# Two-layer attention and mLSTM trunk: q and k of three pieces of four turned by VectorE in 32x32 blocks and through DRAM instead of by TensorE transposes

## The chip, the cores and the metric

The kernel runs on one core of one Trainium2 chip. The metric is the device time of one execution in microseconds (us). The same kernel was run three times: the median is 1334.58 us, the runs lie between 1334.22 and 1334.67. One further execution was recorded by the hardware profiler: it took 1334.56 us, of which 1332.5 us is the span of the trace (first to last recorded instruction).

## The reference

The program is a decoder trunk of two layers over 512 tokens of 1024 channels, in float32. Each layer normalises x, multiplies it with one wide matrix, and feeds the parts to two branches: differential attention with rotary positions, and a chunkwise mLSTM. Both branches are gated, projected, merged and added to x.

```python
proj = rmsnorm(x, norm_g) @ w_in
aq, ak, av, az, bqk, bv, bi, bf, bo, bz, ga, gb = jnp.split(proj, idx, axis=-1)
q = rope(rmsnorm(two_map_heads(aq), q_norm_g), cos, sin)   # 8 heads x 2 maps x 512 tokens x 64
k = rope(rmsnorm(two_map_heads(ak), k_norm_g), cos, sin)
...
sc = jnp.einsum('bhqrd,bhkrd->bhrqk', qb, k) * scale       # causal, softmax over k, two maps r
p = jax.nn.softmax(jnp.where(causal, sc, -jnp.inf), axis=-1)
a = p[:, :, 0] - lam * p[:, :, 1]
oa = rmsnorm(a @ v, attn_norm_g) * (1 - lam_init) * silu(az)
...
u = sigmoid(ga) * (oa @ w_out_a) + sigmoid(gb) * (hb @ w_out_b)
x = x + u @ w_o
```

What the change touches is the way from `aq`, `ak` to the operands of the score product: in the projection a token is a partition, since norm and rotary turn work along a head's 64 features; in the score product the feature has to be the partition. So q and k (4 pieces `c` of two heads each, of q and k together 512 columns) are turned once in every layer.

## The kernel before

**Arithmetic.** Each float32 factor is split into a high part that TensorE takes as its reduced float32 (`wh`, `hh`) and a low rest (`wl`, `hl`); a product is three matmuls (`mm3`, L507): high by high, high by low, low by high. Weights arrive by SyncE's (SP) DMAs as pieces of 128x1024 (`load`, L480, tile `wr`); `prep` (L505) makes `wh` on ScalarE (ACT, a cast) and `wl` on VectorE (DVE, a subtraction).

**Order.** All operations are first recorded (`Recorder`, L103), then ordered by a list scheduler with its own costs and many tuned numbers (`schedule` L272, table `TUNE` L38), and then issued in that order (L441, which is why every row of the profile bears this line). What tells rows apart are the names of the tiles. `TUNE["order"]` gives the order in which the pieces of the projections reach TensorE; other numbers bias when an operation is picked.

**A piece of q and k** (`tok_piece` L708 with `h_tok` L744): for each of four tiles of 128 tokens, the tokens' columns of `hh`, `hl` are the stationary operand (128 contiguous columns) and the 512 columns of the weights move; 8 k-steps of 3 matmuls go to one PSUM tile `qk`, of which the ring `acc` has four for everything that is projected. A piece `c` holds q and k of heads 2c and 2c+1.

**After each tile** (`qk_done` L827): ACT or DVE sum the squares per head and map (`sq`, `qss`); DVE multiplies with a table of cosines and with one of sines in two halves (`ctab`, `stab`: q's and k's gains are in them) and adds (`rot`). After each second tile `rq`, the inverse root mean square, is made. `qk_back` (L883) scales the k half of `rot` by it (ACT in tiles 0 and 2 by four activations of 64 columns, DVE in tiles 1 and 3); q is not scaled, its `rq` is a factor inside the softmax.

**The turn** (`back`, L892): TensorE transposes `rot` in four 128x128 blocks into a PSUM tile `qkt`; ACT casts q's and k's high parts out of it (6 casts of 64x256) and DVE subtracts the low parts (4 of 64x256). High and low part of q lie in one tile of 128 partitions (64 and 64), k's high part twice beside `kl`, half of which is zeroed by GpSimd (POOL, a memset of 64x1024). `back` is deferred by `TUNE["qkt"]` steps after the tile.

**Scores and softmax** (`attn_head` L1161, `qk` L1165): for each head and query block j two matmuls per map give `sc`; DVE adds the causal mask, takes the maximum, multiplies it with -`rq`, and ACT makes the exponentials with `scale=rq` and that bias.

**Start.** `rope_tables` (L538) makes cosines and sines of 4x32 angles per partition from the positions (`posi`), mostly on DVE (`ang`, `rn`, `rnh`), and `layer_consts` (L634) multiplies gains into them: 4 operations for `ctab`, 4 for `stab`, each 128x128.

**Decay tables** (`decay` L1299, `expm` L1314): broadcast rows `dd` and `em` come from DRAM by SP's queue. POOL issues 16 DMAs of weights (`ws_wo`, `wt_wo`) and otherwise only memsets.

Of the kernel before, what the change touches and what calls it, by code (L numbers as in the profile page):

```python
# [42 lines left out]
    ),  # L43
    "qkt": 5,
    "gct": 15,
    "gls": 6,
    "glf": 5,
    "attn": (1, 5, 5, 8, 9, 13, 15, 16, 19, 24),
    "a0": 23,
    "ap": 18,  # L50
    "a4": 7,
    "ml": (1, 9, 11, 12, 13, 28),
# [3 lines left out]
    "margin": 72.0,  # L56
    "pemargin": 171.8,
    "wait": 333.1,
    "swpen": 701284048.1,
    "smargin": 51.6,  # L60
    "pwait": 0.8,
    "wdiff": 3673.3,
    "wsp": 4,
    "kact": (0, 2),
    "qsq": (1, 3),
    "foldA": (2, 3, 5),
    "foldM": (0, 1, 2, 3, 4, 7),
    "foldD": (0, 1, 2, 3, 4, 5, 6, 7),
# [3 lines left out]
    "acl": 12,  # L72
    "gateA": 9,
    "gateM": 0,
    "actp": (0, 2, 3),
    "m0": 218,
    "mp": 15,
    "m4": 11,
    "slots": 20,
    "bias": {'av': 27450.0, 'msp_a': -4350.0, 'wl': 2400.0, 'wo': -3700.0, 'woh': -4650.0, 'ht': 29150.0, 'taz': -4050.0, 'ga': 16050.0, 'gt': -8800.0, 'p': -300.0, 'wo1_P': 23900.0, 'out_0_dram': -5900.0, 'p5_wo': -4950.0, 'rot': 12650.0, 'dq': -4400.0, 'oa': 450.0, 'dd': 30900.0, 'num': 20100.0, 'ld': -4700.0, 'ws1_wo': -1200.0, 'gw': -1100.0, 'hl': -350.0, 'sc': -1400.0, 'uz': -3750.0, 'mk': 7250.0, 'sbz': 550.0, 'az': 10300.0, 'posi': -650.0, 'msl_d': 1650.0, 's1_wo': 1700.0, 'wob': 50.0, 'msh_d': 6450.0, 'sq': -1600.0, 'warm': 3150.0, 'bo': -400.0, 'sdl': 200.0, 'ml': 15800.0, 'fo_b': 11200.0, 'ws0_wo': -900.0, 'wt1_wo': 1300.0, 'pb': 2000.0, 'sbo': 5350.0, 'qkt': 2000.0, 'junk': 6150.0, 'ulZ': 7650.0, 'bv': 650.0, 'bqk': -1750.0, 'uh': -3950.0, 'ms_b': -1550.0, 'gi': 1000.0, 'ob': 250.0, 'uy': 1750.0, 'gcol': -750.0, 'ms': 11250.0, 'cosv': -4100.0, 'ms_a': 1450.0, 'ones': 2450.0, 'msh_b': 6650.0, 'x1d': -1650.0, 'qt': 1100.0, 'qk0_2x': -6300.0, 'fb_a': 4650.0, 'saz': 900.0, 'xr': -2300.0, 'fb_b': 900.0, 'wo0_P': 450.0, 'qk1_0x': 1950.0, 'fb_d': -5800.0, 'msh_a': 2700.0, 'ulA': -150.0, 'ang': 150.0, 'rnh': 1400.0, 'gft': 6600.0, 'gct': 200.0, 'gc': -300.0, 'mql': -1200.0, 'rows': 150.0, 'kl': -700.0, 'posf': -150.0, 'zw': 2400.0, 'qk1_2x': -3000.0, 'gf': 450.0, 'qk0_0x': -50.0, 'uhY': 7150.0, 'qs': 3050.0, 'qy': 250.0, 'ul': -500.0, 'msl_a': 2800.0, 'uhZ': 7800.0, 'lneps': -950.0, 'gm': -4350.0, 'lq': 450.0, 'x': -3700.0, 'eps': -700.0, 'sgb': 150.0, 'wr': -400.0, 'wt0_wo': -300.0, 'stab': 8000.0, 'xn': 1200.0, 'qss': 150.0, 'den': 2000.0, 'msl_b': 950.0, 'rn': -150.0, 'glf': 900.0, 'ss': 4250.0, 'bz': -100.0, 'sdh': -200.0, 'em': -250.0, 'uhB': 850.0, 'rq': 250.0, 'sinv': -1650.0},  # L80
    "drain": 251.9,
    "risk": 295.5,
    "late": 912.7,
# [19 lines left out]
class Recorder:  # L103
# [39 lines left out]
    def region(self, ap):  # L143
# [4 lines left out]
        if k not in self.regions:  # L148
            free = math.prod(k[0][1:])
            p0, np_ = ap.offset // free, pat[0][1]  # L150
# [121 lines left out]
    def schedule(self):  # L272
# [65 lines left out]
        while len(order) < n:  # L338
# [54 lines left out]
            if o["fn"] == "dma_start":  # L393
                size = 4.0
                for x in list(o["a"][0].shape):
                    size *= x
                go = s + c if e == "POOL" else s
                dma = max(dma, go) + size / self.rate(o)
                end[i] = max(dma, go) + 2000.0
# [45 lines left out]
def kernel(ctx, tc, x, pos, wp, wg, cst, par, pb, ngb, out):  # L445
# [52 lines left out]

    xcur = big.tile([P, NT, D], F32, tag="big", name="x0")
# [35 lines left out]
    cosv = cp.tile([P, NT, 32], F32, name="cosv")  # L535
    sinv = cp.tile([P, NT, 32], F32, name="sinv")

    def rope_tables():  # L538
        NF = NT * 32
# [4 lines left out]
        posf = small(NT, "posf")  # L544
# [81 lines left out]
    def layer_events(l):  # L626
# [7 lines left out]
        def layer_consts():  # L634
# [3 lines left out]
            stab = cp.tile([P, NT, 2, 64], F32, tag="stab", name=f"stab{l}")  # L638
            for i in range(2):
                g = pbt[:, B_QK + 64 * i : B_QK + 64 * i + 64]  # L640
                f8 = 8.0 if i else 1.0
                for hf in range(2):
                    gh = g[:, 32 * hf : 32 * hf + 32]
                    go = g[:, 32 * (1 - hf) : 32 * (1 - hf) + 32]
                    V.scalar_tensor_tensor(ctab[:, :, i, 32 * hf : 32 * hf + 32], cosv, f8, gh.unsqueeze(1).to_broadcast([P, NT, 32]), ALU.mult, ALU.mult)
                    V.scalar_tensor_tensor(
                        stab[:, :, i, 32 * hf : 32 * hf + 32], sinv, -f8 if hf == 0 else f8, go.unsqueeze(1).to_broadcast([P, NT, 32]), ALU.mult, ALU.mult
                    )
            st["ctab"], st["stab"] = ctab, stab
# [177 lines left out]
        def qk_done(c, tt, acc):  # L827
# [27 lines left out]
            ctab, stab = st["ctab"], st["stab"]  # L855
            V.tensor_tensor(q4, a4, ctab[:, tt].unsqueeze(2).to_broadcast([P, 2, 4, 64]), ALU.mult)
            for hf in range(2):
                o = 32 * hf
                V.tensor_tensor(
                    s4[:, :, :, o : o + 32],  # L860
                    a4[:, :, :, 32 - o : 64 - o],
                    stab[:, tt, :, o : o + 32].unsqueeze(2).to_broadcast([P, 2, 4, 32]),
                    ALU.mult,
                )
            V.tensor_tensor(rq, rq, r2, ALU.add)
            st[("rot", tt % 2)] = rq
            if tt % 2 == 0:
                return
# [13 lines left out]

        def qk_back(c, tt, rq):  # L883
            k3 = rq[:, 256:512].rearrange("p (g d) -> p g d", d=64)
            rk = st[("rq", c)][:, tt, 4:8].unsqueeze(2).to_broadcast([P, 4, 64])
            if tt in TUNE["kact"]:
                for g in range(4):
                    A.activation(k3[:, g, :], k3[:, g, :], AF.Copy, scale=st[("rq", c)][:, tt, 4 + g : 5 + g])
            else:
                V.tensor_tensor(k3, k3, rk, ALU.mult)  # L890
# [750 lines left out]
```

## Time and profile before

| what | value |
|---|---|
| median of 3 runs | 1334.58 us (1334.22 to 1334.67) |
| profiled execution / its span | 1334.56 us / 1332.5 us |
| TensorE (PE) matmuls | 1325.0 us busy, 99% of the span, x6200 |
| weight loads of TensorE (PEld) | 1095.0 us, 82% |
| VectorE (DVE) | 1018.0 us, 76% |
| ScalarE (ACT) | 907.8 us, 68% |
| GpSimd (POOL) | 36.9 us, 3% |
| bytes moved by DMA | 148.14 MB, 111 GB/s |

Busy times are those of recorded instructions. A matmul's record covers its passage through the array, so successive matmuls overlap: the rate is read from start to start, not from a record's length. "Idle before" of a group is the time its engine waited ahead of it, with the releaser of most of it.

### The profile page before, as it was taken

The page shows a single profiled execution, that of the slowest core. Times are in us where ns is not written, and L with a number is a line of the kernel's source. Part 1 is how long each engine was busy: PE and PEld are TensorE (multiplying, and loading weights), DVE is VectorE, ACT ScalarE, POOL GpSimd, SP SyncE. Part 2 cuts the span into 40 slices and gives each one's busy share as a digit, 9 for nine tenths or more (in the row PEclk, how much of TensorE's full clock was granted, in tenths as well). Part 3 has the DMA queues.
Part 4 walks back from the last instruction along what each step waited for, and adds up shares of the span by engine and source line. Part 5 has one row for each costly group of instructions (what it writes and reads, how often), then busy time and mean ns, then how long its engine had stood idle before and what let it go on. Part 6 is the DMA issues. An engine that isn't in the chain of part 4 may idle for free.

```text
span 1332.5 us, 17532 instructions
## 1 busy us (share of the span) xinstructions
PE 1325.0 (99%) x6200; PEld 1095.0 (82%) x6200; DVE 1018.0 (76%) x1846; ACT 907.8 (68%) x1836; POOL 36.9 (3%) x44
## 2 busy tenths in 40 slices
PE   9999999999999999999999999999999999999998
PEld 7888888888888888888788888888888888888886
DVE  7898899786259968755888988997852699687566
ACT  6878798877247858743667787889762489687343
POOL 1000000000000000000200000000000000000000
PEclk9999999999999999999999999999999999999999
DMA  5222222223333443554833122222332344354646
GB/s 188 87 67 78 80 83 64 91 79 99 95 103 112 149 123 113 146 155 128 248 112 95 49 95 64 79 76 83 82 112 79 128 119 141 99 135 135 170 122 182
DMA packets 51272, 148.14 MB, mean 111 GB/s; under 512 B 6096, under 2 KB 12880, under 8 KB 51184
## 3 DMA queue, kind: packets, MB, share of 16 engines
q1 hardware_dynamic: 48880, 138.63, 32.9%
q0 software_dynamic: 2304, 8.39, 3.6%
q8 instruction: 49, 0.80, 0.2%
q14 instruction: 39, 0.32, 0.1%
HBM read 142.74 MB, written 4.26 MB: 110 GB/s over the span
## 4 chain that ended last, share of the span: by engine, by line
PE 98%; ACT 1%; DMA 0%; SPq 0%; DVE 0%; issue 0%; DVEq 0%
PE qk L441 13%; PE av L441 9%; PE az L441 7%; PE bv L441 7%; PE bqk L441 7%; PE bz L441 7%; PE bo L441 7%; PE gb L441 7%; PE ga L441 7%; PE woa L441 7%; PE wob L441 7%; PE wo_P L441 6%; PE sc L441 3%; PE num L441 2%; PE ms L441 1%; PE ut L441 1%
## 5 line engine op out<-in xcount | busy, mean ns | idle before, releaser
L441 ACT CAST wh<-wr 128x1024 fp32r<-128x1024 f32 (+1 forms) x206 | 214.8, 1045 | 190.0 <-PE ga L441 36.3
L441 DVE TENSOR_TENSOR wl<-wr,wh 128x1024 fp32r<-128x1024 f32 (+1 forms) x208 | 248.9, 1200 | 99.7 <-ACT wh L441 98.9
L441 PE MATMUL qk<-wh,hh 128*128 128x512 f32 x256 | 96.1, 401 | 0.5 <-ACT hh L441 0.5
L441 PE MATMUL qk<-wh,hl 128*128 128x512 f32 x256 | 95.3, 400 | 0.1
L441 PE MATMUL qk<-wl,hh 128*128 128x512 f32 x256 | 94.8, 396 | 0.5 <-DVE wl L441 0.5
L441 ACT ACTIVATE p<-sc,mx,rq 128x128 f32<-128x128 f32 (+3 forms) x128 | 78.8, 618 | 16.2 <-DVE mx L441 15.6
L441 PE MATMUL woa<-oa,wh 128*128 128x512 f32 x256 | 87.8, 390 | 0.0
L440 ACT ACT_TABLE_LOAD x65 | 83.4, 1283 | 1.1
L441 PE MATMUL wob<-ob,wh 128*128 128x512 f32 x256 | 83.4, 389 | 0.0
L441 PEld LDWEIGHTS qk<-wl,hh 128*128 128x128 f32 x256 | 48.0, 188 | 10.2 <-DVE wl L441 0.9
L441 PEld LDWEIGHTS wob<-ob,wh 128*128 128x128 f32 x256 | 48.1, 188 | 10.1
L441 PEld LDWEIGHTS qk<-wh,hl 128*128 128x128 f32 x256 | 48.0, 188 | 10.0 <-DVE hl L441 0.4
L441 PEld LDWEIGHTS qk<-wh,hh 128*128 128x128 f32 x256 | 47.7, 188 | 10.0 <-ACT hh L441 0.9
L441 PEld LDWEIGHTS woa<-oa,wh 128*128 128x128 f32 x256 | 47.8, 188 | 9.7
L441 DVE TENSOR_REDUCE mx<-sc 128x2 f32<-128x256 f32 (+1 forms) x64 | 52.5, 821 | 1.1
L441 PE MATMUL bqk<-hh,wl 128*128 128x512 f32 x128 | 50.3, 393 | 0.0
L441 PE MATMUL bo<-hh,wl 128*128 128x512 f32 x128 | 50.2, 392 | 0.0
L441 PE MATMUL bo<-hl,wh 128*128 128x512 f32 x128 | 50.1, 391 | 0.0
L441 PE MATMUL bo<-hh,wh 128*128 128x512 f32 x128 | 50.0, 391 | 0.0
L441 PE MATMUL bqk<-hl,wh 128*128 128x512 f32 x128 | 50.0, 393 | 0.0
L441 PE MATMUL az<-hh,wh 128*128 128x512 f32 x128 | 49.8, 397 | 0.0
L441 PE MATMUL gb<-hl,wh 128*128 128x512 f32 x128 | 49.8, 392 | 0.0
(309 smaller groups left out, 3695.9 us busy)
## 6 DMA issues: line engine op xcount, KB each, us to landing
wr<-in_wp_dram SPq DMA_DIRECT2D x204, 512.0 KB, 3.5
ws_wo<-in_wp_dram POOLq DMA_DIRECT2D x12, 512.0 KB, 6.8
dd<-rows SPq DMA_DIRECT2D x16, 256.0 KB, 4.3
em<-rows SPq DMA_DIRECT2D x16, 256.0 KB, 4.0
dd<-rows SPq DMA_DIRECT2D x16, 192.0 KB, 4.8
x<-in_x_dram SPq DMA_DIRECT2D x4, 512.0 KB, 7.4
dd<-rows SPq DMA_DIRECT2D x16, 128.0 KB, 6.0
ws_wo<-in_wp_dram SPq DMA_DIRECT2D x4, 512.0 KB, 5.2
```

Of the source, the lines that this page charges most:

```text
L440: self.tc.keep_in_program_order(self.nc.scalar.preload_act_table_set(self.SET_NAME[o["load"]]))
L441: self.tc.keep_in_program_order(getattr(o["e"], o["fn"])(*o["a"], **o["k"]))
```

## The change

For pieces c = 1, 2, 3 of both layers TensorE's transposes are gone; c = 0 keeps them (`turn`).

- The stationary operand takes every fourth token (`h_perm`): partition p of tile tt is token 4p+tt. Its 128 columns lie 16 bytes apart in place of 4.
- q is scaled by `rq` as k is (`qk_back`, ACT 8 activations of 128x64 in tiles 0, 1 and 2, DVE one 128x512 in tile 3), for c = 0 too. q gets a minus sign in the tables; so the mask is subtracted, a minimum replaces the maximum, and the exponential has `scale=-1.0`: the multiplication of the maximum goes.
- DVE transposes the two 256-column halves of each `rot` in blocks of 32x32, with a strided output, into `tr0`, `tr1`, so that after four tiles 128 tokens of a feature follow each other.
- POOL's queue writes them to `scr` in DRAM (feature by token; 8 writes of 32x8x128, 128 KB each) and reads them with features on partitions: 4 reads into `re` (float32) and 6 straight into the high parts, converted on the way (64x2x512, 256 KB each). DVE subtracts 4 low parts of 64x1024.
- A second set of tables for the permuted tokens: angles, cosines and sines are made for 8x32 in place of 4x32, the first piece's tables lie in a scratch tile `tab`, the positions come in the other order by 4 small DMAs of SP. The sine product is one operation in place of two.
- The loads of `dd` and `em` go from SP's queue to POOL's.
- The order of the pieces and all tuned numbers are new (the first pieces: `qk0 av0 gate az0 qk1` before, `qk0 qk1 az0 gate av0` now); the three lists of heads whose sums of squares are folded to 64 partitions change (`foldA`, `foldM`, `foldD`). Rings `wr`, `wh`, `wl` keep their sizes.

Instructions in the program, before and after: PE 6202 and 6102, DVE 1840 and 1718, ACT 1574 and 1574, POOL 20 and 208, SP 345 and 269 (POOL and SP: DMAs and memsets).

```diff
     "order": (
-        "qk0 av0 gate az0 qk1 az1 az2 av1 qk2 az3 az4 qk3 az6 ga3 az5 ga5 ga4 ga2 az7 bqk7 bv0 bqk4 bqk1 "
+        "qk0 qk1 az0 gate av0 av1 az2 az1 qk2 az3 az4 qk3 az5 bqk7 ga6 ga5 ga7 az6 az7 ga3 bv0 bo0 ga2 "
...
-    "qkt": 5,
+    "qkt": 9,
...
+    "qq": 2,
...
-    "kact": (0, 2),
+    "kact": (0, 1, 2),
...
-    posi = cp.tile([P, NT], I32, name="posi")
+    posi = cp.tile([P, 2 * NT], I32, name="posi")
...
-        SY.dma_start(posi, pos)
+        SY.dma_start(posi[:, :NT], pos)
+        for c in range(NT):
+            SY.dma_start(posi[32 * c : 32 * c + 32, NT:], pos.rearrange("(d t) c -> c d t", t=NT)[c])
...
-        NF = NT * 32
+        NF = 2 * NT * 32
...
-        for tt in range(NT):
+        for tt in range(2 * NT):
             V.tensor_scalar(ang[:, tt * 32 : tt * 32 + 32], ct[:, C_IF : C_IF + 32], posf[:, tt : tt + 1], None, ALU.mult)
...
+            st["tabs"] = ((first[:, 0], first[:, 1]), (ctab, stab))
...
+                    for w, (tc_, ts_) in enumerate(st["tabs"]):
+                        ns = slice(w * NT, w * NT + NT)
+                        V.scalar_tensor_tensor(tc_[:, :, i, ds], cosv[:, ns], f8, gh, ALU.mult, ALU.mult)
+                        V.scalar_tensor_tensor(ts_[:, :, i, ds], sinv[:, ns], -f8 if hf == 0 else f8, go, ALU.mult, ALU.mult)
...
+        def h_perm(k, tt):
+            return st["hh"][:, k, tt::NT], st["hl"][:, k, tt::NT]
...
         def qk_back(c, tt, rq):
+            r8 = rq.rearrange("p (g d) -> p g d", d=64)
...
-                for g in range(4):
-                    A.activation(k3[:, g, :], k3[:, g, :], AF.Copy, scale=st[("rq", c)][:, tt, 4 + g : 5 + g])
+                for g in range(8):
+                    A.activation(r8[:, g, :], r8[:, g, :], AF.Copy, scale=st[("rq", c)][:, tt, g : g + 1])
...
+            for i in range(2):
+                V.transpose(st["tr"][i].rearrange("p (a r) -> p a r", r=P)[:, :, tt::NT], rq[:, 256 * i : 256 * i + 256])
+            if tt < NT - 1:
+                return
+            scr = dram.tile([S, S], F32, name=f"scr{l}_{c}")
+            for i in range(2):
+                for b in range(NT):
+                    QW.dma_start(
+                        scr[256 * i : 256 * i + 256, P * b : P * b + P].rearrange("(a b) r -> b a r", b=32),
+                        st["tr"][i][32 * b : 32 * b + 32].rearrange("p (a r) -> p a r", r=P),
+                    )
...
             def back():
-                pst = ps_tr.tile([P, 4, P], F32, tag="tr", name=f"qkt{l}_{c}_{tt}")
-                for g in range(4):
-                    T.transpose(pst[:, g, :], rq[:, g * P : (g + 1) * P], ident)
...
+                for e, q, k, kl, a, b in ((0, q0, k0, kl0, L, H), (1, q1, k1, kl1, H, L)):
+                    r = q2w(f"re{e}{l}_{c}", F32).rearrange("p (g t) -> p g t", g=2)
+                    QR.dma_start(r[a], s5[0, e])
+                    G.dma_start(q[a], s5[0, e])
+                    QR.dma_start(r[b], s5[1, e])
+                    G.dma_start(k[a], s5[1, e])
+                    G.dma_start(k[b], s5[1, e])
+                    V.tensor_tensor(q[b], r[a], q[a].bitcast(F32), ALU.subtract)
+                    V.tensor_tensor(kl[a], r[b], k[b].bitcast(F32), ALU.subtract)
...
-                V.tensor_tensor(dg, dg, mask_a.unsqueeze(1).to_broadcast([P, 2, P]), ALU.add)
+                V.tensor_tensor(dg, dg, mask_a.unsqueeze(1).to_broadcast([P, 2, P]), ALU.subtract)
...
-                V.tensor_reduce(mx, sc[:, :, :n], AX.X, ALU.max)
...
-                V.scalar_tensor_tensor(mx, mx, -1.0, rq, ALU.mult, ALU.mult)
+                V.tensor_reduce(mx, sc[:, :, :n], AX.X, ALU.min)
...
-                    SY.dma_start(dd[:, OFF[i] : OFF[i] + n], rows[h : h + 1, P * i :].to_broadcast([P, n]))
+                    G.dma_start(dd[:, OFF[i] : OFF[i] + n], rows[h : h + 1, P * i :].to_broadcast([P, n]))
...
-                SY.dma_start(em, rows[8 + h : 9 + h, :].to_broadcast([P, S]))
+                G.dma_start(em, rows[8 + h : 9 + h, :].to_broadcast([P, S]))
...
-            ps["qk%d" % c] = tok("qk", c, h_tok, qk_done)
+            ps["qk%d" % c] = tok("qk", c, h_perm if c else h_tok, qk_done)
```

With `qq` at 2 both `QW` and `QR` are POOL's queue (`G`).

The order on TensorE at the end of the first piece of layer 0, before: in the names `qk0_0_3` is layer 0, piece 0, tile 3, the number behind the last underscore counts tiles.

```order
L441 MATMUL qk0_0_3_137<-wh3_139,hl0_115 128x512
L441 MATMUL qkt0_0_0_183<-ct_94,rot0_0_0_164 128x128 x2
L441 MATMUL qk0_0_3_137<-wh3_139,hh0_114 128x512
L441 MATMUL qk0_0_3_137<-wl3_140,hh0_114 128x512
L441 MATMUL qk0_0_3_137<-wh3_139,hl0_115 128x512
L441 MATMUL av0_0_0_179<-wh4_153,hh0_114 128x512
```

The same place now.

```order
L457 MATMUL qk0_0_3_137<-wh3_139,hh0_114 128x512
L457 MATMUL qk0_0_3_137<-wl3_140,hh0_114 128x512
L457 MATMUL qk0_0_3_137<-wh3_139,hl0_115 128x512
L457 MATMUL qk0_1_0_180<-wh4_154,hh0_114 128x512
L457 MATMUL qk0_1_0_180<-wl4_155,hh0_114 128x512
```

The second piece of q and k stands where the first of v stood, and no transposes stand between the matmuls. The piece that follows still needs the first of the four PSUM tiles of `qk0_0` back.

The order on POOL around piece c = 2 of layer 0, before: between its memsets POOL issues nothing.

```order
L441 MEMSET kl00_1_279 64x1024
L441 MEMSET kl10_1_280 64x1024
L441 MEMSET kl00_2_411 64x1024
L441 MEMSET kl10_2_412 64x1024
L441 MEMSET kl00_3_492 64x1024
L441 MEMSET kl10_3_493 64x1024
```

The same place now (`qk0_2x` is the tile of q's and k's high and low parts of this piece).

```order
L457 DMA scr0_2_434<-tr00_2_423 32x8x128 x4
L457 DMA scr0_2_434<-tr10_2_424 32x8x128 x4
L457 DMA qk0_2x_412<-scr0_2_434 64x2x512 x2
L457 DMA re00_2_460<-scr0_2_434 64x2x512
L457 DMA re10_2_461<-scr0_2_434 64x2x512
L457 MEMSET kl00_3_491 64x1024
L457 MEMSET kl10_3_492 64x1024
L457 DMA re00_2_460<-scr0_2_434 64x2x512
L457 DMA qk0_2x_412<-scr0_2_434 64x2x512
L457 DMA re10_2_461<-scr0_2_434 64x2x512
L457 DMA qk0_2x_412<-scr0_2_434 64x2x512 x3
```

All 18 transfers of a piece stand in one queue, and the two memsets for the next piece between them.

More of the change, by code (lines that the diff above doesn't have):

```diff
@@ L71 @@
     "prods": 'P1 P5 P3 P6 P2 P7 P4',
[L72 to L75, printed above, removed]
+    "acl": 14,
+    "gateA": 1,
+    "gateM": 4,
+    "actp": (0, 1, 2, 3),
     "m0": 218,
[L77 to L78 removed]
+    "mp": 17,
+    "m4": 23,
     "slots": 20,
[L80 removed]
@@ L84 @@
+    "drain": 1559.5,
+    "risk": 203.8,
+    "late": 61.0,
 }
@@ L149, in region @@
             free = math.prod(k[0][1:])
+            if t.name.startswith("scr"):
+                off = [ap.offset]
+                for st, n in pat:
+                    off = [o + st * i for o in off for i in (range(n) if st > 1 else range(0, n, 32))]
+                quad = mask = 0
+                for o in off:
+                    quad |= 1 << o // free // 256
+                    mask |= 1 << o % free // 32
+                self.regions[k] = quad, mask
+                return (t.name,) + self.regions[k]
             p0, np_ = ap.offset // free, pat[0][1]
@@ L398, in schedule @@
                 dma = max(dma, go) + size / self.rate(o)
-                end[i] = max(dma, go) + 2000.0
+                end[i] = max(dma, go) + (4000.0 if o["a"][1].tensor.name.startswith("rows") else 2500.0)
             for t in o["tiles"]:
@@ new lines, in qk_back @@
+                for g in range(8):
+                    A.activation(r8[:, g, :], r8[:, g, :], AF.Copy, scale=st[("rq", c)][:, tt, g : g + 1])
+            else:
+                V.tensor_tensor(r8, r8, st[("rq", c)][:, tt, 0:8].unsqueeze(2).to_broadcast([P, 8, 64]), ALU.mult)
+            if c == 0:
+                defer(TUNE["qkt"], lambda: turn(c, tt, rq))
+                return
+            if tt == 0:
+                take(2)
+                st["tr"] = [q2w(f"tr{i}{l}_{c}", F32) for i in range(2)]
@@ L1478, in add_up, with way, wtile, src_of @@
             G.dma_start(chains[n, a], source(l, n, 1, 1 if t == "T2" else 0, a), accum_op=ALU.add)
+    per = len(layers[0][0])
+    def way(i):
+        key = pieces[i][1]
+        if key == "gate" or key[0] == "seven" and key[2] not in ("P1", "P2", "P3"):
+            return "s"
+        for w in "ab":
+            lo, hi, step, ph = TUNE["w" + w]
+            if lo <= i % per < hi and i % step in ((ph,) if isinstance(ph, int) else ph):
+                return w
+        return "s"
+    def wtile(name, dt):
+        tag = name.rstrip("0123456789")
+        return wpool.tile([P, 1024], dt, tag=tag, bufs=2 if tag == "wr" else 3, name=name)
+    def src_of(i):
+        l, key = pieces[i]
+        if key == "gate":
+            return wg[l]
+        if key[0] == "seven":
+            _, n, prod, a = key
+            return source(l, n, *{"P1": (0, 0), "P2": (1, 0), "P3": (1, 1)}[prod], a)
+        return wp[l, KIDX[key]]
     def load(i):
@@ L1510, in prep @@
         if key == "gate":
-            wh = wpool.tile([P, 1024], F32R, tag="wh", name=f"wh{i}")
+            wh = wtile(f"wh{i}", F32R)
             w4 = wh.rearrange("p (k a n) -> p k a n", k=KT, a=2)
@@ L1547 @@
             starts[i](state["t"])
-        for a in range(3):
-            load(i + a)
+        for a in range(max(3, TUNE["wahead"])):
+            if a < 3 or i + a < len(pieces) and way(i + a) == "a":
+                load(i + a)
         for a in range(TUNE["acl"] + 1):
```

150 lines of the change are left out of this document (82 added, 68 removed), and 6 rows, old and new, of the table TUNE.

## The prediction

> **What bounds the kernel now.** I read the page first: busy shares, then the chain that ended last.
>
> ```profile
> PE 1325.0 (99%) x6200; PEld 1095.0 (82%) x6200; DVE 1018.0 (76%) x1846; ACT 907.8 (68%) x1836; POOL 36.9 (3%) x44
> ...
> PE 98%; ACT 1%; DMA 0%; SPq 0%; DVE 0%; issue 0%; DVEq 0%
> ```
>
> TensorE is the chain: 98% of it. The waits of TensorE by what it waited for say how little of that is waiting:
>
> ```profile
> PE warm L441 <- DVE ml L441: 1.6, 1, 1.6
> PE qk L441 <- ACT hh L441: 0.5, 1, 0.5
> PE ht L441 <- DVE junk L441: 0.5, 2, 0.3
> PE qk L441 <- DVE wl L441: 0.5, 1, 0.5
> ```
>
> These four come to 3.1 us, all at the start. The windows of the stretches in which q and k are made and of the start (busy time of PE, PEld, DVE, ACT, POOL, then granted clock, DMA share, GB/s):
>
> ```profile
> 0.00:35.00 35.00, 31.78 (x143) 24.88 (x144) 26.79 (x73) 21.53 (x52) 4.94 (x9) 1.00 0.53 179
> 100.00:200.00 100.00, 100.00 (x492) 82.39 (x491) 89.72 (x200) 84.38 (x233) 1.90 (x2) 1.00 0.25 81
> 200.00:300.00 100.00, 100.00 (x487) 82.40 (x487) 85.32 (x183) 82.74 (x201) 1.90 (x2) 1.00 0.24 78
> ```
>
> PE never stops between 100 and 300 us at a granted clock of 1.00, DVE stands at 90% and 85% beside it. So the time is the sum of what TensorE issues, plus what it would newly wait for. What an instruction costs there is read from starts, on TensorE's timeline around a group of four transposes:
>
> ```profile
> 218.96 0.39 PE L441 MATMUL az<-hl,wh 128*128 128x512 f32 x1
> 219.19 0.40 PE L441 MATMUL az<-hh,wl 128*128 128x512 f32 x1
> 219.42 0.60 PE L441 MATMUL qkt<-ct,rot 128*128 128x128 f32 x4
> 219.78 0.48 PE L441 MATMUL az<-hh,wh 128*128 128x512 f32 x1
> 220.09 0.39 PE L441 MATMUL az<-hl,wh 128*128 128x512 f32 x1
> 220.32 0.39 PE L441 MATMUL az<-hh,wl 128*128 128x512 f32 x1
> ```
>
> A matmul of 512 columns starts 0.23 after another (218.96 to 219.19 to 219.42). From 219.19 to 220.32 lie 1.13 us with three of them (0.68) and four transposes: 0.45, or 0.112 each.
>
> **The change part by part.**
>
> *Transposes.* 128 become 32: 96 x 0.112 = 10.75 us off TensorE's queue. All of it is on the path, as nothing else holds TensorE there. Bounds by the rounding of the starts: 10.3 to 11.2.
>
> *Folded heads.* The lists of folded heads change the 512-wide matmuls with ones by -10, +4 and +2: -4 x 0.23 = -0.9.
>
> *DVE and ACT.* The rows that go and the nearest ones of what comes (mean ns of one behind the comma, or min/median/max):
>
> ```profile
> L441 ACT CAST ks<-qkt x64: 360/367/371, 106.7 to 897.8; 64x256 fp32r<-64x256 f32 x64
> L441 DVE TENSOR_TENSOR qs<-qkt,qs x32: 417/422/428, 106.3 to 897.0; 64x256 fp32r<-64x256 f32 x32
> L441 DVE SCALAR_TENSOR_TENSOR mx<-mx,rq 128x2 f32<-128x2 f32 x64 | 9.9, 155 | 0.7
> L441 ACT ACTIVATE rot<-rot,rq 128x64 f32<-128x64 f32 x64 | 17.4, 340 | 1.9 <-DVE rq L441 1.6
> L441 DVE TENSOR_TENSOR wl<-wr,wh 128x1024 fp32r<-128x1024 f32 x200 | 243.7, 1221 | 98.5 <-ACT wh L441 97.7
> L441 DVE TENSOR_TENSOR sq<-qk,stab 128x256 f32<-128x256 f32 x64 | 25.5, 416 | 0.3
> ```
>
> DVE loses 96 subtractions (40.5) and 64 products of the maximum (9.9); it gains 24 subtractions of 1024 columns by the `wl` row (29.3) and 48 block transposes of 128x256, which the trace does not have: by the nearest row of that size, `sq`, 0.42 each (20), at worst twice that for the strided output (40), at best half (10). Net about -1 us, -11 to +19. ACT loses 144 casts (52.8) and gains 128 scalings (43.5): -9. Both fit under TensorE, so I take nothing for them in the sum; what would end the cover is in the rivals.
>
> *The start.* The first piece's rotary products now wait for more tables. DVE's timeline, then TensorE's first matmul behind the first piece:
>
> ```profile
> 20.90 0.57 DVE L441 TENSOR_SCALAR ang<-ct,posf 128x32 f32<-128x32 f32 x3
> ...
> 26.13 0.29 DVE L441 SCALAR_TENSOR_TENSOR ang<-rnh,ang 128x128 f32<-128x128 f32 x1
> ...
> 30.17 0.29 DVE L441 SCALAR_TENSOR_TENSOR stab<-sinv,pb 128x128 f32<-128x128 f32 x1 [0.35 <-ACT sinv L441]
> 30.38 0.28 DVE L441 SCALAR_TENSOR_TENSOR ctab<-cosv,pb 128x128 f32<-128x128 f32 x1
> ...
> 32.39 0.75 DVE L441 TENSOR_TENSOR sq<-qk,stab 128x256 f32<-128x256 f32 x2
> 33.05 1.22 DVE L441 TENSOR_TENSOR wl<-wr,wh 128x1024 fp32r<-128x1024 f32 x1
> ```
>
> ```profile
> 36.12 0.40 PE L441 MATMUL av<-wh,hh 128*128 128x512 f32 x1
> ```
>
> Tile 0 of the first piece gave its PSUM back at 33.1, 3 us before `av` wanted it (the ring has four tiles). Ahead of that point DVE now has 4 more angle rows (0.57/3 = 0.19 each, 0.8), about 15 rows of 256 columns in place of 128 (0.42 by `sq` for 0.29: 2.0), 8 more table rows (0.20 from start to start, 1.6) and one more `wl` (1.2): 5.6 us. Release at 38.7 against 36.1: **2.6 us** of waiting, all on the path. Bounds: 0, if DVE's gaps (here 0.35) and a better place of the `wl` take it up; 5.6, if something else is late with it. The 4 small loads of positions are on SP:
>
> ```profile
> 4.54 0.60 SPq L441 DMA_DIRECT2D posi<-in_pos_dram  x1
> ...
> 11.62 7.10 SPq L441 DMA_DIRECT2D wr<-in_wp_dram  x3
> ```
>
> They add 4 x 0.60 = 2.4 us to SP's queue ahead of a weight piece that is used some 10 us after it was issued here; the cover is those 10 us, and without it 2.4 us would be paid once.
>
> *The way through DRAM.* From the last matmul of a piece, DVE ends its tail, POOL issues 18 DMAs and 2 memsets, the last read lands, DVE subtracts, and only then the first score of head 2c can start. In before, c = 2, the tail shows on TensorE's and DVE's timelines:
>
> ```profile
> 171.21 0.39 PE L441 MATMUL qk<-wh,hl 128*128 128x512 f32 x1
> ```
>
> ```profile
> 181.47 0.41 DVE L441 TENSOR_TENSOR rot<-rot,rq 128x256 f32<-128x256 f32 x1
> ```
>
> 10.7 us to the end of the last scaling; a scaling of twice the columns (+0.3) and two block transposes (0.8) make it 11.8. For POOL's DMAs there are only loads of weights, 512 KB each: POOL's timeline, the time to landing of this tile, and the table of DMA issues (last number: median us to landing):
>
> ```profile
> 560.64 1.00 POOL L441 DMA_DIRECT2D ws_wo<-in_wp_dram  x1 [143.16 <-DVE dq L441]
> 561.79 0.87 POOL L441 DMA_DIRECT2D ws_wo<-in_wp_dram  x1 [0.15 <-issue]
> ...
> 20.44 0.95 POOL L441 MEMSET kl<- 64x1024 f32 x1 [15.75 <-DVE junk L441]
> ...
> DMA to landing us min/median/max: 4.4/6.1/8.4
> ```
>
> ```profile
> ws_wo<-in_wp_dram POOLq DMA_DIRECT2D x12, 512.0 KB, 6.8
> ...
> em<-rows SPq DMA_DIRECT2D x16, 256.0 KB, 4.0
> ...
> ws_wo<-in_wp_dram SPq DMA_DIRECT2D x4, 512.0 KB, 5.2
> ```
>
> One DMA holds POOL 0.87 to 1.15 (from start to start); I take 1.01, 0.86 and the gap of 0.15. The same 512 KB take 5.2 from SP and 6.8 from POOL, 1.6 more; 256 KB take 4.0 from SP, so 5.6 from POOL. Chain: 11.8 + 17 x 1.01 + 2 x 0.95 + 5.6 + 1.3 (the subtraction) = 37.8 us. Cover on TensorE for c = 2, counted in the new order from the last `qk` matmul to the first `sc` of head 4: 154 matmuls of 512 columns (35.0) and 13 narrower ones, 2,816 columns together (1.2): 36.2. So 1.6 us late in each layer, **3.2** in both. Bounds: with 0.87 and 4.4 the chain is 34.2 and hidden (0), with 1.15 and 6.8 it is 41.4, 5.2 late, 10.4 in both. Piece 1 has a cover of some 55 us and piece 3 of 46.9: hidden, even at the upper bound. Behind the waiting subtractions DVE's queue has piece 3's sums of squares and rotary products, which hold PSUM tiles, and two `wl`; TensorE needs the first of those 28 rows after the score, so the score comes first.
>
> The Trainium skill ("DMA: Bandwidth & Descriptors", Specifications) gives first-byte latencies of about 1 us for GpSimd's path and 0.6 for SyncE's, 0.4 apart where the rows have 1.6. By the page the chain would be 36.6 and 0.4 late, and the whole time, as an estimate, 1326.3.
>
> `dd` and `em` on POOL: 80 DMAs x 1.01 = 81 us on an engine that is busy 37 of 1332; they land 1.6 later and are asked for long before use. Nothing; if issued late behind a piece's 18, a few us on DVE first.
>
> **Sum**, against the profiled execution (1334.56, 0.02 from the median): 1334.56 - 10.75 - 0.9 + 2.6 + 3.2 = **1328.7 us**. All bounds at their good end give 1322.4, all at their bad end 1339.4.
>
> **The rivals.**
>
> *A: strided weight loads are slow, slower.* The weight loads of the projection and of the transposes:
>
> ```profile
> L441 PEld LDWEIGHTS qk<-wl,hh 128*128 128x128 f32 x256 | 48.0, 188 | 10.2 <-DVE wl L441 0.9
> ```
>
> 188 ns of 227 is shown, but the four transposes at 112 ns each had a load each, so a load occupies 112 at most. It decides once a load passes 227, twice that. Three times, 336, would add 0.109 x 576 (three pieces of 96 matmuls, two layers) = 63 us: about 1391. For it: no load in the trace has that stride. Against it: the room of a factor of two. The Trainium skill ("SBUF — State Buffer", the section on the DMA port swizzle) says that SBUF has 16-byte lines, that full bandwidth needs two hits in a line and each crossing pays; at 16 bytes each value is in a line of its own. That speaks for this rival, without a size; no row here shows it. Chance 0.06.
>
> *B: POOL is late with its DMAs, slower.* A write has 256 rows of 512 bytes where `ws_wo` has 128 of 4 KB. If POOL's time goes by rows, the 8 writes take 1.73 each: 11.8 + 8 x 1.73 + 9 x 1.15 + 1.9 + 6.8 + 1.3 = 46.0, 9.8 late, 19.6 in both layers: 1325.5 + 19.6 = 1345.1. It ends above 1337.2 once a piece is 5.9 late, at 1.26 us per DMA. Against it: the order leaves 36 us of cover. Chance 0.14.
>
> *C: the gain goes to DVE or ACT.* DVE at 90% with a burst of transposes and subtractions behind a DMA wait: weights' `wl` or the `p` of the softmax come late by a fraction of a us at many places, 6 us in all: 1334.6. For: the windows. Against: DVE's and ACT's sums fall. Chance 0.14.
>
> *D: more than the sum.* No wait at the start or at piece 2, and the 3.1 us of waits at the start shrink by the new order: 1334.56 - 10.75 - 0.9 - 2 = 1321. Chance 0.06.
>
> **How the numbers follow.** The forecast has 0.60 and, by itself, a range from 1322.4 to 1331.9. 0.2% is 2.7 us, what a measurement of this kernel can tell from no change. Faster: forecast and D, 0.66. Same: C, 0.14. Slower: A and B, 0.20. The range goes from D's side, 1320, to 1342, which takes in C, the sum's bad end of 1339.4 and the milder half of B; A and the rest of B, some 0.15, are left out.
>
> **What would show it.** Right: 32 `qkt` transposes, PE at 99%; a wait of 2 to 3 us of the second piece's first matmul for a `qk` tile near 36 us; a wait of `sc` before heads 4 of 1 to 2 us on a subtraction or DMA; 0.227 from start to start in the second piece as in the first. Wrong: a longer spacing there (A); waits of over 5 us before `sc` and POOL at over 1.3 us per DMA (B); many short waits of PE on `wl`, `p` or `uh` (C).

## The result and the profile after

The changed kernel takes 1357.17 us (median of 4 runs, 1355.95 to 1360.38) against 1334.49 of the kernel before: a ratio of 1.0171, interval 1.0159 to 1.0184. It is 22.7 us slower; 1328.7 was forecast. The profiled execution took 1356.59 us and has a span of 1354.8 (before: 1332.5).

The page of the changed kernel, busy shares and the chain that ended last:

```profile
PE 1328.9 (98%) x6100; PEld 1118.2 (83%) x6100; DVE 1019.0 (75%) x1724; ACT 873.0 (64%) x1836; POOL 144.0 (11%) x232
...
PE 77%; DVE 8%; DMA 7%; ACT 5%; issue 1%; POOL 1%; SPq 0%; DVEq 0%; ACTq 0%; POOLq 0%
```

TensorE issues 100 matmuls less and is no longer the whole chain: 98% has become 77%, the rest is other engines' work that it waited for. VectorE's busy time is what it was (1018.0) and ScalarE's is lower (907.8), so neither is fuller than before; GpSimd has more to do (144.0 for 36.9), but is busy 11% only. TensorE's longest waits, by what it waited for (us in total, times, longest); all of them together come to 21.6 us, where they were 3.8 before:

```profile
PE av L457 <- ACT av L457: 3.6, 2, 2.3
PE av L457 <- DVE wl L457: 2.2, 2, 1.3
PE ga L457 <- DVE wl L457: 2.2, 2, 1.2
PE sc L457 <- DMA qk_2x<-scr: 2.0, 1, 2.0
PE warm L457 <- DVE ml L457: 1.6, 1, 1.6
PE sc L457 <- DVE kl L457: 1.6, 1, 1.6
...
PE gt L457 <- DVE sq L457: 1.2, 1, 1.2
PE ut L457 <- DVE kl L457: 1.2, 1, 1.2
```

Of these only `warm` stood there before. The waits are many, short and for different things: `sc` waits for the way through DRAM (3.6), the others for weights (`wl`), for splits of v (`av`), for the rotary work of the second piece (`sq`) and for the turn of the first (`kl` of `ut`). The windows of two of the stretches shown before (PE, PEld, DVE, ACT, POOL, clock, DMA share, GB/s):

```profile
100.00:200.00 100.00, 97.47 (x461) 84.56 (x460) 85.59 (x170) 71.35 (x188) 5.79 (x10) 1.00 0.35 93
200.00:300.00 100.00, 96.84 (x459) 82.53 (x458) 85.06 (x158) 73.39 (x192) 19.30 (x32) 1.00 0.66 154
```

TensorE stood at 100.00 in both windows and now misses 2.5 and 3.2 us, while VectorE is no busier (89.72 and 85.32 before). More is missing at the start of each layer's attention half (3.6 from 35 to 100 us, 4.2 from 700 to 800). The gated half of the first layer, 300 to 400 us, is still at 100.00.

### The profile page after: what moved, and what is told of

It reads as the page before. It is cut to its first block, busy times and chain, and to the rows that moved or that the text cites. A ratio compares the mean times of both kernels' runs of the same rounds, so it can differ in the third digit from the quotient of the medians.

```text
span 1354.8 us, 17584 instructions
## 1 busy us (share of the span) xinstructions
PE 1328.9 (98%) x6100; PEld 1118.2 (83%) x6100; DVE 1019.0 (75%) x1724; ACT 873.0 (64%) x1836; POOL 144.0 (11%) x232
## 3 DMA queue, kind: packets, MB, share of 16 engines
q1 hardware_dynamic: 37936, 123.95, 28.7%
## 4 chain that ended last, share of the span: by engine, by line
PE 77%; DVE 8%; DMA 7%; ACT 5%; issue 1%; POOL 1%; SPq 0%; DVEq 0%; ACTq 0%; POOLq 0%
PE qk L457 10%; PE bo L457 6%; PE bv L457 6%; PE av L457 6%; PE wob L457 6%; PE gb L457 6%; PE bz L457 6%; PE wo_P L457 6%; PE woa L457 5%; PE bqk L457 5%; PE ga L457 3%; DMA wr<-in_wp_dram 3%; PE az L457 2%; PE sc L457 2%; PE num L457 2%; DVE wl L457 2%
## 5 line engine op out<-in xcount | busy, mean ns | idle before, releaser
L457 ACT ACTIVATE p<-sc,mx 128x128 f32<-128x128 f32 (+3 forms) x128 | 67.5, 529 | 25.8 <-DVE mx L457 23.1
L457 PEld LDWEIGHTS qk<-wh,hh 128*128 128x128 f32 x256 | 67.2, 281 | 5.5 <-ACT wh L457 1.0
L457 PEld LDWEIGHTS qk<-wl,hh 128*128 128x128 f32 x256 | 67.4, 280 | 3.8 <-DVE wl L457 0.9
L457 PEld LDWEIGHTS qk<-wh,hl 128*128 128x128 f32 x256 | 67.1, 280 | 3.4 <-DVE hl L457 0.4
L457 POOL DMA_DIRECT2D scr<-tr x48 | 28.1, 594 | 385.1 <-DVE tr L457 385.1
L457 ACT ACTIVATE rot<-rot,rq 128x64 f32<-128x64 f32 x192 | 51.4, 343 | 4.1 <-DVE rq L457 4.1
L457 PE MATMUL ga<-hh,wl 128*128 128x512 f32 x128 | 50.9, 397 | 2.2 <-DVE wl L457 2.2
L457 PE MATMUL av<-wl,hh 128*128 128x512 f32 x128 | 49.9, 402 | 2.2 <-DVE wl L457 2.2
L457 PE MATMUL ga<-hh,wh 128*128 128x512 f32 x128 | 51.3, 401 | 0.7 <-DVE saz L457 0.7
L457 POOL DMA_DIRECT2D dd<-rows x64 | 34.8, 550 | 160.0 <-PE ut L457 109.1
## 6 DMA issues: line engine op xcount, KB each, us to landing
qk_2x<-scr POOLq DMA_DIRECT2D x12, 256.0 KB, 10.5
```

Of the source, the lines that this page charges most:

```text
L457: self.tc.keep_in_program_order(getattr(o["e"], o["fn"])(*o["a"], **o["k"]))
```

## The experiments

The order in which a kernel's instructions are issued is made by its planner from the code and the table `TUNE`; whoever edits either gets another order. Each experiment was timed beside the kernel before, whose medians there lie between 1334.4 and 1334.9; a ratio is to the one beside it. Two kinds of experiment follow: some exchange code and table, others keep the order of issue of the changed kernel instruction for instruction and change at issue what is sent.

**The stride.** E1 takes contiguous columns in the changed kernel; E2 puts the stride alone into the kernel before.

```diff
-            ps["qk%d" % c] = tok("qk", c, h_perm if c else h_tok, qk_done)
+            ps["qk%d" % c] = tok("qk", c, h_tok, qk_done)
```

> The changed kernel with the stationary operand of pieces 1 to 3 taken as 128 contiguous columns again, all else and the order the same; q and k then belong to other tokens than the tables and masks say. In the trace of the changed kernel the matmuls of such a piece start 0.235 us apart (53.97 to 55.85) in place of 0.227, and their weight loads pull the mean of the group from 188 to 280 ns. Theory that the stride costs only this spacing: 576 x 0.008 = 4.6 us less, about 1352.5. Rival, that the longer loads also make TensorE start late after every wait: 7 us or more less, 1350 or under. Rival, that the spacing comes from something else in that stretch: 1357, and 0.235 stays.

> The kernel before with the strided stationary operand in pieces 1 to 3 and nothing else; q and k then belong to permuted tokens. Stride theory: 576 x 0.008 = 4.6 us more, about 1339.1. If the spacing in the changed kernel came from its other traffic: 1334.5.

Measured: E1 1352.18 (1.0129, interval 1.0112 to 1.0146), 5.0 us less than the changed kernel; E2 1344.1 (1.0072, interval 1.0057 to 1.0087), 9.7 more than before, twice what was expected. The loads of the changed kernel and of E1, mean ns of one behind the comma:

```profile
L457 PEld LDWEIGHTS qk<-wl,hh 128*128 128x128 f32 x256 | 67.4, 280 | 3.8 <-DVE wl L457 0.9
```

```profile
L457 PEld LDWEIGHTS qk<-wl,hh 128*128 128x128 f32 x256 | 48.0, 188 | 11.4 <-DVE wl L457 1.7
```

With a quarter of the loads still at 188, the strided ones take (4 x 280 - 188)/3 = 311 ns, longer than the 227 between two matmuls. What that costs depends on what stands ahead. TensorE's timeline at a place where a `qk` matmul follows four narrow ones, first before, then in E2:

```profile
76.43 0.60 PE L441 MATMUL ut<-ct,p 128*128 128x128 f32 x4
76.78 0.48 PE L441 MATMUL qk<-wh,hl 128*128 128x512 f32 x1
77.09 0.40 PE L441 MATMUL qk<-wh,hh 128*128 128x512 f32 x1
```

```profile
76.59 0.60 PE L441 MATMUL ut<-ct,p 128*128 128x128 f32 x4
76.94 0.60 PE L441 MATMUL qk<-wh,hl 128*128 128x512 f32 x1
77.38 0.40 PE L441 MATMUL qk<-wh,hh 128*128 128x512 f32 x1
```

Behind the narrow ones the next start comes 0.44 us later in place of 0.31. Counted over all `qk` matmuls of the two traces (a quarter of them, piece 0, not strided), from each start to the next, waits left out: 71 stand behind narrow ones and go from 305 to 399 ns on average, 6.7 us in all; the other 695 go from 230 to 234, 2.8 us. Together that is E2's loss; the expected 4.6 came from the spacing behind wide matmuls alone. The changed kernel has 50 such places, and the same count there, against E13 below, gives 8.6 us. E1's 5.0 is low beside that, but E1 ran at a granted clock of 0.993 to 0.997 and the changed kernel at 0.996 to 0.999, and 0.001 of the time is 1.4 us. So the stride is a loss of 5 to 10 us.

**Code and table exchanged.** E3 is the code before with the table now, E4 the code now with the table before; E7 and E8 cut the table of E3 in two: E7 has the lines of `order`, E8 all from `qkt` on.

```diff
     "order": (
-        "qk0 av0 gate az0 qk1 az1 az2 av1 qk2 az3 az4 qk3 az6 ga3 az5 ga5 ga4 ga2 az7 bqk7 bv0 bqk4 bqk1 "
+        "qk0 qk1 az0 gate av0 av1 az2 az1 qk2 az3 az4 qk3 az5 bqk7 ga6 ga5 ga7 az6 az7 ga3 bv0 bo0 ga2 "
...
-    "qkt": 5,
-    "gct": 15,
+    "qkt": 9,
+    "gct": 16,
...
```

> The code before with the whole table of the changed kernel (order of the pieces, biases, folded heads). Theory that the new waits come from the transfers through DRAM, which hold up weight pieces: the table costs little by itself, 1330 to 1338. Rival, that the new order bunches the work of VectorE and ScalarE and TensorE waits for that: 1345 to 1355 already here.

> The code of the changed kernel with the table of the kernel before. Theory of the transfers: as slow as the changed kernel or slower, 1355 to 1370, as the old order leaves shorter covers for pieces 1 and 2. Rival, the order: the waits for VectorE and ScalarE go and what stays is the sum with the stride, 1330 to 1340.

> The kernel before with only the order of the pieces of the changed kernel; biases, folded heads and all other numbers as before. Theory that the order, with piece 1 of q and k right behind piece 0, bunches VectorE's work: most of the 15.9 us that the whole table cost, 1345 to 1355. Rival, that the biases and folds cost it: 1334 to 1339.

> The counterpart: the kernel before with the biases, folds and all other numbers of the changed kernel, but its own order of the pieces. Order theory: 1334 to 1340. Rival: 1345 to 1355. Both this and the order alone slow, by more than the 15.9 us together, would say that they fit only each other.

Measured: E3 1350.33 (1.0117, interval 1.0102 to 1.0132), E4 1427.86 (1.0699, interval 1.0682 to 1.0717), E7 1363.17 (1.0216, interval 1.0201 to 1.0231), E8 1377.48 (1.0323, interval 1.0307 to 1.0338). The new table costs the old code 15.9 us, without one transfer through DRAM, as the rival had it. The new code needs that table: with the old one it is 93 us slower than before, far above both expectations. And neither half of the table is the culprit, since each alone costs more (28.7 and 43.0) than both, the third outcome that was allowed for E8: the numbers fit each other and one code. TensorE's longest waits in E4:

```profile
PE sc L457 <- ACT p L457: 16.3, 10, 2.5
PE av L457 <- ACT uh L457: 10.6, 3, 4.9
PE sc L457 <- DMA ks<-scr: 5.0, 2, 4.8
PE sc L457 <- DVE kl L457: 4.1, 2, 3.3
```

All waits of E4 come to 61.9 us. The two groups on the transfers and their subtractions (`ks`, `kl`) are 9.1 of them, the softmax (`p`) is the largest with 16.3; that it came late behind the transfers is likely, but was not traced. The other large part is clock: the granted clock was 0.975 over the span of 1426.6 us, 36 us of lost clock, some of which fell into waits (see the last section).

**How many pieces.** E10 and E11 are the code of the changed kernel with no piece through DRAM, with the old and the new table; E9 sends only piece 3, with the old table.

```diff
+PERM = (3,)      # E9; () in E10 and E11
-            if c == 0:
+            if c not in PERM:
                 defer(TUNE["qkt"], lambda: turn(c, tt, rq))
...
-            ps["qk%d" % c] = tok("qk", c, h_perm if c else h_tok, qk_done)
+            ps["qk%d" % c] = tok("qk", c, h_perm if c in PERM else h_tok, qk_done)
```

> The code of the changed kernel with the table before, where only piece 3 goes through DRAM and pieces 1 and 2 are turned by TensorE. In the old order piece 3 has a cover of some 37 us of matmuls. If the loss with the old table (93 us with three pieces) comes from the short covers of pieces 1 and 2: 32 transposes less (3.6), a third of the stride (1.7 more) and 0 to 4 of waiting, 1332 to 1337. If any piece through DRAM unsettles the order: above 1345.

> The same with no piece through DRAM: four pieces turned by TensorE, contiguous loads, old table; what is left of the change is the scaling of q, the sign, the wider tables at the start and dd and em on GpSimd's queue. If these are as cheap as the prediction took them: 1333 to 1338. If they are part of the loss (VectorE at the start, ScalarE's scalings): above 1342.

> No piece through DRAM, with the new table. Theory that the table is the loss in either code: 1346 to 1354, as the code before with it (1350). If the new table fits the new arithmetic better than the old: 1338 to 1344.

Measured: E9 1350.29 (1.0118, interval 1.0101 to 1.0135), E10 1350.26 (1.0116, interval 1.0101 to 1.0131), E11 1367.32 (1.0246, interval 1.0230 to 1.0261). Without the way through DRAM the code still loses 15.9 us under the old table and 32.9 under the new one: the first theory was too low for E9 and E10, both were for E11, and that the old order only lacked covers for pieces 1 and 2 falls. E10 is where it was to be if the scaling of q and the start were part of the loss; as its order is new too, it can't tell those from the order; E15 and the part on the start below come nearer to that. Piece 3 by itself is worth nothing, E9 against E10. Its 32 transposes (3.6) may be paid back by the stride and by these waits, 3.3 us in E9; as the two orders differ, that is only argued:

```profile
PE sc L460 <- DVE kl L460: 3.3, 3, 1.9
```

**The way through DRAM, order kept.** E5 leaves out the 8 writes of a piece and puts a memset in place of each of the 10 reads; E6 keeps the writes and adds for each read a copy of 256 KB of weights within DRAM that nobody waits for. In both, q and k of three pieces are zeros.

```diff
+            if o["fn"] == "dma_start" and o["a"][0].tensor.name.startswith("scr"):
+                continue
+            if o["fn"] == "dma_start" and o["a"][1].tensor.name.startswith("scr"):
+                self.tc.keep_in_program_order(self.nc.gpsimd.memset(o["a"][0].bitcast(F32), 0.0))
+                continue
```

> The changed kernel with the same order of issue, but without the transfers through DRAM: the 8 writes of a piece are left out, and each of the 10 reads is a memset of the same tile on GpSimd (q and k are then zeros). No landing to wait for and no bytes. Theory that the transfers hold up weight pieces and scores: what the changed kernel loses beside the table (15.9) and the stride (5.0), less the transposes' gain (10.7), is 12 us; all of it goes: 1345. Rival, that the new instructions of VectorE and ScalarE (block transposes, scalings, subtractions of 1024 columns) in a queue already full are the loss: 1353 to 1357.

> As the run without the way, but with its bytes: the 8 writes of a piece stay, and beside each memset that stands for a read GpSimd issues a copy of 256 KB of weights within DRAM, which nobody waits for. If the weight pieces behind these bytes are the loss: near the changed kernel, 1353 to 1358. If it is the waiting of scores and subtractions for the landing: near the run without the way, 1344 to 1348.

Measured: E5 1347.41 (1.0093, interval 1.0076 to 1.0110), nearer to the theory's 1345 than to its rival; E6 1349.87 (1.0118, interval 1.0103 to 1.0133), between both. The way costs 9.8 us. Where, shows the chain of waits of the changed kernel in piece 2 of layer 0, up to the second `kl`:

```profile
205.08 1.06 ACT wh L457
206.16 1.24 DVE wl L457
207.42 11.01 DMA wr<-in_wp_dram
218.47 0.04 issue
218.50 1.06 ACT wh L457
219.59 0.98 DVE wl L457
220.57 0.27 issue
220.84 1.23 DVE kl L457
```

A piece of weights needs 11.01 us to land (3.5 in the median before) while the reads of `scr` run, its `wl` comes late on VectorE, and `kl`, which the score needs, stands behind that `wl`. The times to landing of the tile `qk_2x`, and ScalarE's idle time ahead of its casts `wh` until weights landed, in the kernel before, in E5 and in the changed one (us, times):

```profile
DMA to landing us min/median/max: 6.5/10.5/13.2
```

```profile
  DMA wr<-in_wp_dram: 9.9, 7
```

```profile
  DMA wr<-in_wp_dram: 15.7, 8
```

```profile
  DMA wr<-in_wp_dram: 53.7, 22
```

E5 has the changed kernel's order, so the way accounts for 38 us of this idle time, of which TensorE feels a part. In E6 it comes to 18.4 us only: copies within DRAM do not hold weights up as the real reads do, and E6 understates the bytes. How the 9.8 divide between landing and held-up weights stays open.

**Fewer reads.** E12 reads 4 times per piece and lets ScalarE cast the six high parts.

```diff
-                    G.dma_start(q[a], s5[0, e])
+                    A.copy(q[a], r[a])
-                    G.dma_start(k[a], s5[1, e])
-                    G.dma_start(k[b], s5[1, e])
+                    A.copy(k[b], r[b])
+                    A.copy(k[a], r[b])
```

> The changed kernel with 4 reads of a piece in place of 10: the high parts of q and k are cast by ScalarE from the float32 that was read (6 casts of 64x1024 per piece) and not read again. If the bytes read back and their landing (10.5 us to landing for this tile, 6.7 for the float32) are the loss of the way through DRAM (9.8): 3 to 7 us less, 1350 to 1354. If ScalarE's 36 casts of 1.05 us (38 us) come on the path: 1357 or more.

Measured: 1368.29 (1.0252, interval 1.0237 to 1.0267), 11.1 slower than the changed kernel. The reads land sooner (median 4.4 us in place of 6.7), but the planner makes another order of it, and TensorE's longest waits are now these:

```profile
PE av L457 <- ACT av L457: 9.8, 2, 6.1
```

Its waits come to 27.9 us, 6.3 more, and its runs had a granted clock of 0.991 to 0.993, where the changed kernel's had 0.996 to 0.999: 0.006 of the time is 8 us (part of it may lie in waits).

The time is nearer to the second theory than to the first, but since the order moved too, it says little on the casts.

**What is left, order kept.** E13 is E5 with contiguous loads; E14 also leaves out the 48 block transposes; E15 also ScalarE's scalings of q.

```diff
+            if o["eng"] == "DVE" and o["fn"] == "transpose":
+                continue                                      # E14, E15
+            if o["eng"] == "ACT" and o["kind"] == "rot" and o["a"][0].offset % 512 < 256:
+                continue                                      # E15
```

> The changed kernel with the same order of issue, without the transfers through DRAM (memsets in place of the reads) and with contiguous weight loads; q and k are zeros in pieces 1 to 3. If the two costs add: 1347.4 - 5.0 = 1342.4. If they cover each other: 1345 to 1347.

> The same, and without VectorE's 48 block transposes (26 us of VectorE). Theory that VectorE's new work makes the waits that are left (1342.4 against some 1323 for the sum of the instructions): 1332 to 1338. Rival, that the order of issue makes them whatever the work is: 1340 to 1342.

> The same, and without ScalarE's 96 scalings of q (33 us of ScalarE): less work than the kernel before had on VectorE and on ScalarE. If ScalarE's new work makes the waits: 3 to 8 us under the run without block transposes. If the order of issue does: within 2 us of it, and still over 1337.

Measured: E13 1339.79 (1.0038, interval 1.0023 to 1.0053), E14 1338.45 (1.0027, interval 1.0015 to 1.0038), E15 1335.79 (1.0004, interval 0.9995 to 1.0014). E13 is below both expectations, as the stride is dearer than E1 had it. E14 lies at the edge of the first theory (1338), E15 between its two. The page of E15:

```profile
PE 1317.4 (99%) x6100; PEld 1087.1 (81%) x6100; DVE 999.4 (75%) x1676; ACT 851.0 (64%) x1740; POOL 135.0 (10%) x184
```

E15 has less work than the kernel before on TensorE, VectorE and ScalarE, contiguous loads and nothing to wait for from DRAM, and is not faster. Its longest waits:

```profile
PE ga L466 <- DVE wl L466: 2.5, 2, 1.3
PE ms L466 <- DVE dd L466: 1.6, 2, 0.9
PE warm L466 <- DVE ml L466: 1.6, 1, 1.6
PE gt L466 <- DVE sq L466: 1.2, 1, 1.2
PE ut L466 <- DVE kl L466: 1.2, 1, 1.2
```

They are the waits of the changed kernel without those on the way through DRAM: for weights behind other work on VectorE, for the second piece's rotary work and the first piece's turn. All of E15's waits come to 12.7 us, against 3.8 before; behind the first 20 us they are 9.6 against 0.6. E15 is 2.7 us under E14, so ScalarE's scalings have at most a small part. How the 4.0 us from E13 to E15 divide is not firm: the runs of E14 go from 1336.46 at a granted clock of 1.000 to 1339.44 at 0.996, those of E15 from 1334.35 to 1337.84 likewise. No version beat the kernel before.

## Why the prediction was wrong

With the order kept, each step is what the run loses beside the one ahead of it; the last is what E15 has over the prediction's sum of instructions, 1334.56 - 10.75 - 0.9 = 1322.9.

| step | us | from |
|---|---|---|
| way through DRAM | 9.8 | changed kernel - E5 |
| stride | 7.6 (5.0 with the way, E1) | E5 - E13 |
| block transposes | 1.3, within the scatter of the runs | E13 - E14 |
| scalings of q | 2.7, as uncertain | E14 - E15 |
| order of issue and what is left | 12.9 | E15 - 1322.9 |

- **The step that failed** is one that the sum did not have. The prediction took over from the profile before that "PE never stops" and gave the new order of issue no term. That a planned order leaves 3.8 us of waits is a property of that order with that code: none of the seven runs with another pairing (E3, E4, E7 to E11) lost under 15.9, whichever half was exchanged. When all other causes that were tried are taken out, E15 still has 12.9 us over the sum. Its trace (of a run of 1336.52, 13.6 over) shows what they are: 8.9 us more of TensorE's waits than before, 1.8 us of granted clock (0.95 from 60 to 80 us and 0.96 from 80 to 100, 1.00 before), and 2.9 that were not placed. Rival C put 6 us on just such waits ("many short waits"), as the price of fuller engines; the engines are not fuller, and E14 with E15 give those only 4.0. So the order is found by taking all else out, and by E3, where only the table was changed. Some 1.6 us of `ms` on `dd` may belong to the move of `dd` to POOL instead. Whether a longer search would find an order without these waits for the new code, no run shows.
- **Transposes**, 10.75: 32 are left, as forecast; no run measured the saving alone.
- **The start**, 2.6: the wait for a `qk` tile is not there. The second piece begins with the matmul at 37.41, without a gap:

```profile
37.18 0.40 PE L457 MATMUL qk<-wh,hl 128*128 128x512 f32 x1
37.41 0.40 PE L457 MATMUL qk<-wh,hh 128*128 128x512 f32 x1
37.66 0.39 PE L457 MATMUL qk<-wl,hh 128*128 128x512 f32 x1
```

VectorE gave the first tile back at 37.04, where 38.7 was forecast, and TensorE wanted it at 37.4, not at 36.1. The wider tables are hardly behind the later waits of `gt` and `ut` (70 and 78 us) either, for VectorE, the third number behind the comma, was busy half of the time in between:

```profile
45.00:50.00 5.00, 5.00 (x23) 4.70 (x23) 2.40 (x4) 4.35 (x22) 0.00 (x0) 1.00 0.00 0
50.00:55.00 5.00, 5.00 (x24) 4.96 (x23) 3.09 (x8) 4.05 (x14) 0.00 (x0) 1.00 0.06 12
```
- **The way through DRAM**, 3.2 of waiting for piece 2: the two waits of `sc` are 1.6 and 2.0, 3.6 together, so the sum held, but by luck: its terms did not. POOL issues faster than by the row of the weights' loads, the reads land later, and the tail on VectorE takes 15.0 us, from 182.0 to 197.0, in place of 11.8:

```profile
L457 POOL DMA_DIRECT2D qk_2x<-scr x12: 581/604/627, 202.1 to 877.6; - x12
```

0.60 us per DMA in place of 1.01, 10.5 to landing in place of 5.6. What the step missed is the rest of the 9.8, some 6 us, for which the chain shows one source: weights that land behind the reads.
- **Rival A**, the stride: right in kind, and left out of the sum. Its threshold (a load over 227) was passed at 311, but a load that is 84 ns too long cost 5 to 8 ns behind a wide matmul and some 0.1 us behind narrow ones, not 84 or 109 at each: 7.6 us and not 63. The Trainium skill ("SBUF — State Buffer", the section on the DMA port swizzle) has the right sign, and the trace agrees: loads of one value per 16-byte line took 311 ns for 188. **Rival B** is refuted: POOL's time does not go by rows, the writes of 256 rows took 0.58 each. It was to end slower, as the kernel did, but for another reason.
- **VectorE and ScalarE**, taken at nothing: the block transposes took 0.54 each (26.1 us in all) where 0.42 was estimated. VectorE's busy time rose by 1.0 where -1 was forecast; ScalarE's fell by 34.8 where 9 was forecast, so the sum of rows missed part of it.

## What to carry to other kernels

Where one engine is busy 99% of the time in a planned order, the order is the asset: an edit that saves 10 us of that engine's instructions loses if the order has to be made anew and leaves 9 us more of short waits, so such a change is to be priced with a term for the order, and tried first with the order kept. A cover found for a long transfer is not free: what moves forward to make it is work for the engines beside, and the transfers' bytes go in front of others'. Leaving out at issue one kind of instruction after the other, with the order kept, takes a loss apart where exchanging settings only shows that they belong together. Even so, compare the granted clocks first: 0.001 of them was 1.4 us here, as much as the smaller steps.

## What the runs showed of the hardware

The granted clock fell after short waits. TensorE's timeline and windows of the changed kernel around 80 us (in the windows the clock is the number behind POOL's count):

```profile
77.92 0.30 PE L457 MATMUL ut<-ct,p 128*128 128x128 f32 x1 [1.20 <-DVE kl L457]
79.08 0.59 PE L457 MATMUL av<-wl,hh 128*128 128x512 f32 x1 [0.87 <-DVE wl L457]
...
80.31 0.63 PE L457 MATMUL av<-wl,hh 128*128 128x512 f32 x1
80.74 0.63 PE L457 MATMUL av<-wh,hh 128*128 128x512 f32 x1
```

```profile
75.00:80.00 5.00, 2.93 (x12) 1.97 (x11) 4.81 (x11) 4.90 (x23) 0.00 (x0) 0.94 0.01 2
80.00:85.00 5.00, 5.00 (x18) 3.94 (x17) 5.00 (x14) 4.99 (x15) 0.00 (x0) 0.72 0.40 113
```

After waits of 1.20 and 0.87 us the matmuls stood 0.43 apart instead of 0.23, at a granted clock of 0.72 over 5 us: 1.4 us lost beside the waits themselves. The Trainium skill ("TensorE: Matmul & The Clock Gate", Part 1, the HAM clock gate) puts the fall of the clock behind an idle window of about 3.4 us; here two gaps of 2.1 us together, in a stretch of 5 us in which TensorE was busy 2.93, were enough.

In E4 the waits are longer, and so is the fall:

```profile
150.00:175.00 25.00, 14.32 (x41) 10.53 (x42) 19.18 (x37) 13.38 (x31) 0.94 (x1) 0.52 0.13 44
```

The clock stayed near half, 0.52, for 25 us in which TensorE was busy 14.32 and its longest wait was 3.3. So a wait can cost more than its own length. Over whole spans the clock goes with the waits, though not strictly: 1.000 before with 3.8 us of them, 0.999 in the changed kernel with 21.6, 0.996 in E8 with 30.6, 0.991 in E12 with 27.9, 0.975 in E4 with 61.9.
